# Last output projection with tokens across partitions: the residual turned by VectorE and 128-byte transfers, the norm per partition, token halves in turn

## The chip, the cores and the metric

The kernel runs on one core of one Trainium2 chip. The metric is the device time of one execution in microseconds (us). Five engines work side by side on that core and wait for one another through semaphores: TensorE (PE, with its weight loads as PEld), VectorE (DVE), ScalarE (ACT), GpSimd (POOL, hardly used here) and SyncE (SP), which issues the DMA transfers. All transfers, from whichever queue, are carried by the core's 16 DMA engines.

## What is computed

The reference is a decoder of two blocks on 256 tokens with width 2048, all in float32. The first block has one layer of chunked attention with a relative bias, one layer of attention with forget gates, and an RMS norm. The second block puts 16 meta tokens in front of the 256, normalises, and runs two hybrid layers. The change is at the end of the second of these. Cut to what matters:

```python
def _layer_norm(x, g, b):
    mu = jnp.mean(xf, axis=-1, keepdims=True)
    var = jnp.mean(jnp.square(xf - mu), axis=-1, keepdims=True)
    return (xf - mu) * lax.rsqrt(var + LN_EPS) * g + b

def _hybrid_layer(h, ...):          # h: tokens x 2048
    proj = h @ w_in                 # 2048 x 5632
    ...                             # y_conv 512, y_attn 1024, y_lru 512, each gated
    mixed = jnp.concatenate([y_conv, y_attn, y_lru], axis=-1) @ w_out   # 2048 x 2048
    return _layer_norm(DEEPNORM_ALPHA * h + mixed, ln_post_g, ln_post_b)

for l in range(DEPTH):              # 2 layers
    h = _hybrid_layer(h, ...)
return h[:, N_META:]                # the 16 meta tokens are dropped
```

## The kernel before

**Layout.** The residual stream lies in `X`, two tiles of 128 partitions with eight feature tiles each: features across partitions, tokens along the free axis (`tk(X, m, c0, c1)`, L393, is feature tile m). Every product is made in a split form, for more than the precision of one pass: a float32 operand is cut into a high part (rounded to the fp32r format by ScalarE) and a low part (the rest, by VectorE), and the products high x high, high x low and low x high are added in PSUM. `mm2` (L432) does that with two matmuls when there are 256 tokens: the high weight against high and low tokens side by side (512 columns), and the low weight against the high tokens (256 columns). The two column halves of the 512 wide accumulator are added when it is read.

**The weight stream.** All weights come from one tensor, cut into chunks of 2048 columns, two halves of 1024 each (512 KB). `Prog.run` (L322) writes the order of the work out by hand. For half i it emits, in this order: ScalarE's high part of half i+4 (`high`), VectorE's low part of half i+3 (`low`) and, right after it, the load on SP of half i+7 (`load`, into the buffer which that low part has set free); then the matmuls of half i; then what the chunk that ended before it left to do (`flush`, its evacuation); then one step of each task (`step`). A chunk with `need` first drains the named tasks. Five buffers hold prepared weights (`LOOK` + 2) and four hold raw ones (`RAWB`). Instructions of one engine run in the order in which they are emitted, so a wait holds up all that stands behind it on that engine, SP's queue included.

**Tasks.** The attention, the convolution, the recurrence and the gating are generators that are advanced between the halves. A task that yields `"fill"` is run as filler whenever an estimate of VectorE's clock is less than 2.5 us ahead of TensorE's. `get` and `take` hand out five PSUM banks, `put` gives one back, and three further banks are the accumulators `acc`.

**The last projection (L1705 to L1757, layer 1).** 16 output tiles of 128 features. For the first six the product is cut in two: first the half of the inputs that is ready early (`mix_lo`), for all six, with the pointwise convolution (`pw_mm`) between them, and then the other half (`mix_hi`). The other ten tiles are whole chunks. `ev_o` (L1709) adds the accumulator to the scaled residual, in two passes, and calls `post` of `boundary` (L1045), which subtracts an estimate of the mean, squares, and adds up the sums of the values and of the squares over the feature tiles (`sumd`, `ssum`).

**The end (L1763 to L1791).** The sums go over the partitions by four matmuls with a tile of ones. ScalarE and VectorE make the mean and the inverse deviation as tiles of 128 x 256, the same in each partition. Then every feature tile has its mean subtracted, is multiplied by the inverse deviation (both on VectorE, with groups of two or four tiles in one instruction), and gets the gain and the offset, which lie per partition there, by ScalarE or VectorE. Six stores carry it out.

## Time and profile before

| | us |
|---|---|
| median of 3 runs (2672.63 to 2674.19) | 2673.63 |
| the profiled execution, its own time | 2672.44 |
| span of the profiled execution, first to last instruction | 2670.7 |
| busy in it: PE / DVE / ACT | 2643.2 / 2004.7 / 1501.7 |

The mean granted clock of TensorE is 0.997 of full speed. "Busy" counts the time in which an engine had at least one instruction under way. Matmuls are pipelined, so their times overlap, and the pace is read from start to start. In a row of the timeline the first number is the start in us from the beginning of the span, the second how long the row lasts; `x8` counts merged instructions; a bracket at the end tells how long the engine had stood idle before, and what ended the wait. SPq is SP's queue: the row of a transfer there is its issue and not its flight.

### The profile page before, as it was taken

What the parts mean: (1) busy time and instruction counts of PE and PEld (TensorE: products, weight loads), DVE (VectorE), ACT (ScalarE), POOL (GpSimd) and SP (SyncE); (2) the same over time, 40 slices, a digit from 0 to 9 for tenths busy, and PEclk for the clock granted to TensorE, in tenths of its full rate; (3) what the DMA queues carried; (4) which work ended last, traced back from release to release, by engine and by line L of the source; (5) the groups of instructions that cost most, each with busy time, mean ns of one, the idle gap of its engine ahead of it and who ended that gap; (6) DMA issues with size and microseconds to landing.
All of it is one profiled execution on the core that took longest, in us unless ns stands there. A gap on an engine that the chain in (4) does not pass through costs nothing. (4 is left out here: it accounts for less than half of the span.)

```text
span 2670.7 us, 43856 instructions
## 1 busy us (share of the span) xinstructions
PE 2643.2 (99%) x16914; PEld 2385.1 (89%) x16914; DVE 2004.7 (75%) x3716; ACT 1501.7 (56%) x2326; POOL 3.4 (0%) x20
## 2 busy tenths in 40 slices
PE   9999999999999999999999999999999999999997
PEld 7888888888888888888888888888999999999986
DVE  7777677776765587777777777767799877899867
ACT  6555555555554455554555545644566765756853
POOL 0000000000000000000000000000000000000000
PEclk9999999999999999999999999999999999999998
DMA  7656655555555565555565555565554355554453
GB/s 226 194 175 192 191 176 186 173 192 185 178 181 189 190 199 177 189 177 186 173 193 185 181 185 174 178 203 190 165 186 155 118 164 172 171 172 147 147 171 110
DMA packets 137826, 473.84 MB, mean 177 GB/s; under 512 B 14960, under 2 KB 23568, under 8 KB 137616
## 3 DMA queue, kind: packets, MB, share of 16 engines
q1 hardware_dynamic: 137472, 471.02, 55.2%
q8 instruction: 133, 2.18, 0.3%
q14 instruction: 77, 0.63, 0.1%
q10 hardware_dynamic: 144, 0.01, 0.0%
HBM read 468.84 MB, written 2.13 MB: 176 GB/s over the span
## 5 line engine op out<-in xcount | busy, mean ns | idle before, releaser
L178 ACT CAST w<-raw 128x1024 fp32r<-128x1024 f32 (+1 forms) x874 | 910.5, 1044 | 909.5 <-PE acc L178 661.3
L178 DVE TENSOR_TENSOR w<-raw,w 128x1024 fp32r<-128x1024 f32 (+1 forms) x874 | 1057.0, 1217 | 299.3 <-ACT w L178 298.1
L178 PE MATMUL acc<-hAs1a,w 128*128 128x512 f32 (+1 forms) x768 | 151.7, 339 | 1.1 <-DVE w L178 0.5
L178 PE MATMUL acc<-hAs1b,w 128*128 128x256 f32 (+1 forms) x768 | 150.1, 338 | 1.7 <-DVE w L178 1.7
L178 PE MATMUL acc<-hAs2b,w 128*128 128x256 f32 (+1 forms) x768 | 149.0, 336 | 1.5 <-DVE w L178 1.5
L178 PE MATMUL acc<-hAs2a,w 128*128 128x256 f32 (+1 forms) x768 | 149.7, 337 | 0.0
L178 PEld LDWEIGHTS acc<-hAs1a,w 128*128 128x128 f32 x768 | 122.8, 188 | 18.3 <-DVE w L178 1.8
L178 PEld LDWEIGHTS acc<-hAs2b,w 128*128 128x128 f32 x768 | 123.2, 188 | 17.8 <-issue 1.8
L178 PEld LDWEIGHTS acc<-hAs1b,w 128*128 128x128 f32 x768 | 122.5, 188 | 18.0 <-DVE w L178 2.3
L178 PEld LDWEIGHTS acc<-hAs2a,w 128*128 128x128 f32 x768 | 122.6, 188 | 15.7
L178 ACT ACT_TABLE_LOAD x102 | 130.9, 1283 | 4.4 <-DVE evt L178 1.5
L178 DVE COPY evb<-acc 128x256 f32<-128x256 f32 (+1 forms) x193 | 81.3, 421 | 52.2 <-PE acc L178 52.0
L178 DVE SCALAR_TENSOR_TENSOR rpadw<-agt,pv,rpadw 128x272 f32<-128x272 f32 (+1 forms) x240 | 102.3, 487 | 0.0
L178 PE MATMUL acc<-hbs3b,w 128*128 128x256 f32 (+1 forms) x512 | 100.7, 339 | 0.0
L178 PE MATMUL acc<-hbs3a,w 128*128 128x512 f32 (+1 forms) x512 | 99.6, 337 | 0.0
L178 PE MATMUL acc<-hbs4b,w 128*128 128x256 f32 (+1 forms) x512 | 99.2, 335 | 0.0
L178 PE MATMUL acc<-hbs4a,w 128*128 128x256 f32 (+1 forms) x512 | 99.2, 335 | 0.0
L178 PEld LDWEIGHTS acc<-hbs3a,w 128*128 128x128 f32 x512 | 82.7, 188 | 10.7
L178 PEld LDWEIGHTS acc<-hbs4a,w 128*128 128x128 f32 x512 | 82.5, 188 | 10.9
L178 PEld LDWEIGHTS acc<-hbs4b,w 128*128 128x128 f32 x512 | 82.4, 188 | 10.8
L178 ACT ACTIVATE e<-e,m 128x128 f32<-128x128 f32 (+1 forms) x128 | 57.3, 448 | 61.0 <-DVE m L178 60.7
L178 PEld LDWEIGHTS acc<-hbs3b,w 128*128 128x128 f32 x512 | 81.4, 188 | 10.3
(488 smaller groups left out, 5092.8 us busy)
## 6 DMA issues: line engine op xcount, KB each, us to landing
raw<-in_wstream SPq DMA_DIRECT2D x869, 512.0 KB, 4.4
bias<-in_rel SPq DMA_DIRECT2D x16, 256.0 KB, 5.4
cb<-cumd SPq DMA_DIRECT2D x16, 256.0 KB, 5.0
Xb<-in_xT SPq DMA_DIRECT2D x2, 512.0 KB, 8.4
scrB<-in_lruw SPq DMA_DIRECT2D x2, 512.0 KB, 5.8
tabs<-in_tabs SPq DMA_DIRECT2D x1, 552.0 KB, 6.2
raw<-in_wstream SPq DMA_DIRECT2D x2, 256.0 KB, 5.0
Xa<-in_xT SPq DMA_DIRECT2D x1, 512.0 KB, 7.6
```

The lines of the kernel that those rows point to most:

```text
L178: return fn(*a, **k)
```

## The change

The last projection of the second layer is made with tokens across partitions, in two halves of 128 tokens. The gated inputs become the stationary operand and the weights the moving one, in blocks of 256 output features and two accumulators, one for each token half. For that the residual is turned: `turn_task` transposes every feature tile in blocks of 32 x 32 on VectorE, in place, and `move_task` carries the blocks to their places in a new tile `xt` by 64 transfers from SP, each from 32 partitions to 32 partitions in pieces of 128 bytes; two more transfers copy the gain and the offset into all partitions. An evacuation folds the accumulator into `xt`, takes the mean and variance of its 256 columns with one instruction (`bn_stats`), and multiplies by the gain. The last block of 256 features is computed for the first token half while its weights arrive, and the weights are kept for the second half. At the end mean and deviation are one number per partition; a piece of 512 features takes one pass that makes offset minus mean times gain, and one that applies the deviation. For two pieces of the second half TensorE makes the first of these. The output is stored with tokens across partitions.

The diff, without the unchanged way of layer 0 and the clean-up of `boundary`:

```diff
+    def even(t, c, name):
+        a = slot.tile([P, HS], F32R, tag=t + c, name=name + t + c)
+        off = 48 if c == "b" else 16
+        return a[:, off:off + 4 * 2 * S].rearrange("p (k i n) -> p k i n", k=4, i=2)
...
-                T["M", 2 * i + j] = pairs(sd[i], c, f"mix{i}", L)
+                T["M", 2 * i + j] = even(sd[i], c, "mix") if l else pairs(sd[i], c, f"mix{i}", L)
...
-            pchunk(cq, lambda i=i: T["rg"][:, i, cq:], then=silu_rg if i == 3 else None)
+            pchunk(cq, lambda i=i: T["rg"][:, i, cq:], then=silu_rg if i == 3 else None, spawn=[turn_task] if l and i == 0 else [])
...
-            pchunk(cq, lambda t=t: ag_dst(t), AF.Silu, then=mark(("ag", t)), spawn=[mix_lo, mix_hi] if t == 0 else [])
+            pchunk(cq, lambda t=t: ag_dst(t), AF.Silu, then=mark(("ag", t)), spawn=[mix_lo, mix_hi] if t == 0 else [move_task] if l and t == 7 else [])
...
+    def turn_task():
+        for m in range(16):
+            V.transpose(out=tk(X, m, NM, L), in_=tk(X, m, NM, L))
+            yield "fill"
+
+    def move_task():
+        yield
+        yield
+        last["x"] = [slot.tile([P, HS], F32, tag="s6" + c, name="xt" + c)[:, 0:2048].rearrange("p (t f) -> p t f", t=2) for c in "ab"]
+        for c in range(2):
+            for f in range(4):
+                src = X[c][32 * f:32 * f + 32, :, NM:L].rearrange("p m (t q j) -> p m t q j", t=2, q=4)
+                for q in range(4):
+                    for t in range(2):
+                        dst = last["x"][c][32 * q:32 * q + 32, t].rearrange("p (m f j) -> p m f j", m=8, f=4)
+                        SY.dma_start(out=dst[:, :, f], in_=src[:, :, t, q])
+                yield
+        for k, c in enumerate("ab"):
+            last["gb"[k]] = slot.tile([P, HS], F32, tag="s5" + c, name="row" + c)[:, 0:DM]
+            t = A["rows"]
+            SY.dma_start(out=last["gb"[k]], in_=bass.AP(tensor=t.tensor, offset=t.offset + DM * k, ap=[[0, P], [1, DM]]))
+            yield
...
+        def half_mm(i, t, wt, kt):
+            j, k, m = kt % 4, slice(128 * t, 128 * t + 128), T["M", kt // 4][:, kt % 4]
+            f, e, a = kt == 0, kt == 15, acc[i, t]
+            two = [lambda: TE.matmul(a, m[:, 0, k], wt.both(256 * j, 256), start=f, stop=e),
+                   lambda: TE.matmul(a[:, 256:512], m[:, 1, k], wt.h[:, 256 * j:256 * j + 256], start=False, stop=False)]
+            for x in two if f else two[::-1]:
+                x()
+
+        def mm(i, hh):
+            def f(h, wt):
...
+                if i == 7:
+                    kept.append(wt)
+                for j in range(4):
+                    for t in range(1 if i == 7 else 2):
+                        half_mm(i, t, wt, 8 * hh + 4 * h + j)
+            return f
+
+        def ev(i):
+            def f():
+                for t in range(2):
+                    fold(i, t)
+                    if t:
+                        put(acc[i, t])
+                for t in range(2):
+                    stat(i, t)
+                    gain(i, t)
+            return f
+
+        def fold(i, t):
+            x, a = xt(t, 256 * i, 256), acc[i, t]
+            V.scalar_tensor_tensor(out=x, in0=x, scalar=ALPHA, in1=a[:, :S], op0=ALU.mult, op1=ALU.add)
+            V.tensor_tensor(out=x, in0=x, in1=a[:, S:], op=ALU.add)
+
+        def stat(i, t):
+            V.bn_stats(out=last["bs"][:, t, i], in_=xt(t, 256 * i, 256))
+
+        def gain(i, t):
+            x = xt(t, 256 * i, 256)
+            V.tensor_tensor(out=x, in0=x, in1=last["g"][:, 256 * i:256 * i + 256], op=ALU.mult)
...
+        for i in range(NI):
+            if i == NI - 1:
+                prog.add(Chunk(T["pw_mm"], need=("conv_task",), evac=mark("pw")))
+            add(i, 0, need=("mix_lo",) if i == 0 else ())
+        for i in range(NI):
+            add(i, 1, need=("mix_hi", "move_task") if i == 0 else (), evac=ev(i))
+        for i in range(NI, 8):
+            for hh in range(2):
+                add(i, hh, evac=ev(i) if hh and i < 7 else None)
...
-    b1, b2 = bank(), bank()
...
+    def moments(t):
+        fold(7, t)
+        stat(7, t)
+        V.bn_aggr(out=z[:, t, 0:2], in_=last["bs"][:, t].rearrange("p i c -> p (i c)"))
+        SA.activation(out=z[:, t, 1:2], in_=z[:, t, 1:2], func=AF.Sqrt, scale=1.0, bias=eps[:, 1:2])
+
+    def scales(t):
+        gain(7, t)
+        V.reciprocal(out=z[:, t, 1:2], in_=z[:, t, 1:2])
+        V.scalar_tensor_tensor(out=z[:, t, 2:3], in0=z[:, t, 0:1], scalar=-1.0, in1=z[:, t, 1:2], op0=ALU.mult, op1=ALU.mult)
+
+    def piece(t, c, u=None):
+        w, x = slice(512 * c, 512 * c + 512), xt(t, 512 * c, 512)
+        if u is None:
+            u = B2["wk"].tile([P, 512], F32, tag="pts", name="u", bufs=3)
+            V.scalar_tensor_tensor(out=u, in0=last["g"][:, w], scalar=z[:, t, 2:3], in1=last["b"][:, w], op0=ALU.mult, op1=ALU.add)
+        V.scalar_tensor_tensor(out=x, in0=x, scalar=z[:, t, 1:2], in1=u, op0=ALU.mult, op1=ALU.add)
+        SY.dma_start(out=A["out"][:, t, w], in_=x)
+
+    for kt in range(16):
+        half_mm(7, 1, last["kept"][kt // 4], kt)
+    us = {c: bank() for c in (2, 3)}
+    for c, u in us.items():
+        TE.matmul(u, ident, last["b"][:, 512 * c:512 * c + 512], start=True, stop=False)
+    moments(0)
+    scales(0)
+    for c in range(3):
+        piece(0, c)
+    moments(1)
+    piece(0, 3)
+    scales(1)
+    V.tensor_scalar(out=dg, in0=ident, scalar1=z[:, 1, 2:3], scalar2=None, op0=ALU.mult)
+    for c, u in us.items():
+        TE.matmul(u, dg, last["g"][:, 512 * c:512 * c + 512], start=False, stop=True)
+    for c in range(4):
+        piece(1, c, us.get(c))
```

## Rows read from the trace of the kernel before

**Rows 1.** The page, part 1: busy us (share of span) xinstructions.
```profile
PE 2643.2 (99%) x16914; PEld 2385.1 (89%) x16914; DVE 2004.7 (75%) x3716; ACT 1501.7 (56%) x2326; POOL 3.4 (0%) x20
```

**Rows 2.** Chain that ended last, in order of time: start us, us, what.
```profile
2594.54 55.86 PE acc L178 x320
...
2650.42 0.43 DVE Xb L178
...
2650.88 0.43 DVE Xb L178
...
2665.76 0.32 DVEq L1936
```

**Rows 3.** Timeline, VectorE passes of 256 and 512 columns: start us, us, instruction.
```profile
2614.25 0.42 DVE L178 TENSOR_TENSOR sumd<-sumd,Xa 128x256 f32<-128x256 f32 x1
2614.58 0.42 DVE L178 TENSOR_TENSOR ssum<-ssum,sq 128x256 f32<-128x256 f32 x1
...
2657.15 0.69 DVE L178 TENSOR_TENSOR Xa<-Xa,comb 128x512 f32<-128x512 f32 x1
2657.76 0.69 DVE L178 TENSOR_TENSOR Xa<-Xa,nb 128x512 f32<-128x512 f32 x1
```

**Rows 4.** Groups of VectorE instructions, whole span: xcount | busy us, mean ns.
```profile
L178 DVE TENSOR_TENSOR w<-raw,w 128x1024 fp32r<-128x1024 f32 x866 | 1051.8, 1222 | 296.4 <-ACT w L178 295.2
...
L178 DVE TENSOR_SCALAR anm<-am 128x2 f32<-128x2 f32 x32 | 5.4, 169 | 1.1
...
L178 DVE TENSOR_REDUCE csm<-rpadw 128x256 f32<-128x1024 f32 x1 | 2.0, 1957 | 0.0
...
L178 DVE SCALAR_TENSOR_TENSOR gates<-bank,pv,gates 128x256 f32<-128x256 f32 x4 | 1.9, 484 | 3.3 <-PE bank L178 3.3
```

**Rows 5.** DMA issues by line: xcount, KB each, median us to landing.
```profile
raw<-in_wstream SPq DMA_DIRECT2D x869, 512.0 KB, 4.4
...
out<-Xa SPq DMA_DIRECT2D x2, 256.0 KB, 2.4
```

**Rows 6.** Timeline of SP's queue, two weight loads of the projection's stage.
```profile
2556.51 0.33 SPq L178 DMA_DIRECT2D raw<-in_wstream  x1
...
2561.99 0.33 SPq L178 DMA_DIRECT2D raw<-in_wstream  x1
```

**Rows 7.** Timeline of SP's queue, three of the last issues at the start.
```profile
3.59 0.43 SPq L178 DMA_DIRECT2D Xa<-in_xT  x1
...
4.07 0.69 SPq L178 DMA_DIRECT2D raw<-in_wstream  x1
...
5.61 0.70 SPq L178 DMA_DIRECT2D Xb<-in_xT  x1
```

**Rows 8.** DMA queues in 0:4, 2655:2671, 2600:2625: packets, MB, share of 16 engines.
```profile
q10 hardware_dynamic: 144, 0.01, 2.4%
...
q1 hardware_dynamic: 2144, 2.10, 37.9%
...
q1 hardware_dynamic: 1301, 4.72, 59.3%
```

**Rows 9.** Timeline, TensorE in a v product and the last projection, one fold.
```profile
1126.35 2.94 PE L178 MATMUL accv<-w,hkvs1b 128*128 128x256 f32 x16
...
2577.33 0.95 PE L178 MATMUL acct<-mix1a,w 128*128 128x256 f32 x2 [0.44 <-ACT mix1a L178]
...
2582.43 0.41 DVE L178 SCALAR_TENSOR_TENSOR Xa<-Xa,acct 128x256 f32<-128x256 f32 x1
...
2594.38 1.55 PE L178 MATMUL acc<-mix0a,w 128*128 128x512 f32 x8
```

**Rows 10.** TensorE's last sums; a window after them: busy by engine, PEclk, DMA.
```profile
2652.78 0.59 PE L178 MATMUL bank<-sq,ones 128*128 128x256 f32 x2
...
2657.00:2658.00 1.00, 0.00 (x0) 0.00 (x0) 0.97 (x3) 0.12 (x1) 0.00 (x0) 0.62 0.00 0
```

**Rows 11.** The same view, the stretch between the convolution and the projection.
```profile
2520.00:2551.00 31.00, 30.18 (x248) 27.71 (x248) 24.66 (x29) 26.34 (x46) 0.00 (x0) 1.00 0.46 153
```

More of the change, by code (lines that the diff above doesn't have):

```diff
@@ L1042, in open_block2, with boundary @@
         V.memset(B2["ptm"], 0.0)
-    def boundary(gname, bname, c0, first, move, slots=None, last=False):
+    def boundary(gname, bname, c0, first, slots):
         S_ = {"todo": [], "c": False, "late": []}
@@ L1086, in post @@
         def post(m):
-            if not (last and m == 15):
-                run_late()
+            run_late()
             x = tk(X, m, c0, L)
-            if m == 0 and move:
+            if m == 0:
                 B2["d"] = newp(slots, "d", LW)
@@ L1736, in mm @@
                 for j in range(8):
-                    mm_o(two[m], wt, j, 8 * hh + j, hh == 0 and j == 0, hh == 1 and j == 7)
+                    mm3(two[m][:, :L], wt, j, *msrc(8 * hh + j), hh == 0 and j == 0, hh == 1 and j == 7)
             return mm
@@ L1761, in hybrid_kernel @@
     prog.run()
-    b1, b2 = bank(), bank()
-    for b, u, w in ((b2, sumd[:, NM:], tk(X, 15, NM, L)), (b1, ssum[:, NM:], B2["sq15"][:, NM:])):
-        TE.matmul(b[:, :S], ones, u, start=True, stop=False)
-        TE.matmul(b[:, :S], ones, w, start=False, stop=True)
-    mean, c = (com.tile([P, L], F32, tag=t, name=t)[:, NM:] for t in ("nb", "comb"))
-    SA.activation(out=mean, in_=b2[:, :S], func=AF.Copy, scale=1.0 / DM)
-    SA.activation(out=c, in_=b2[:, :S], func=AF.Square, scale=1.0 / DM)
@@ L1770, in hybrid_kernel @@
[L1770 to L1791 removed]
+    half_mm, fold, stat, gain = last["f"]
```

106 lines of the change are left out of this document (46 added, 60 removed).

## Prediction

> **What bounds the kernel now.** I read the page's busy table first: TensorE is busy for 99% of the span, so a change pays only where TensorE stands still or where something after its last product is shortened [rows 1]. Then the chain of work that ended last: ten output tiles of the last projection run back to back, 320 matmuls in 55.86 us, 5.59 us a tile, up to 2650.40; after that the chain is almost all VectorE, and its last piece ends at 2666.08 [rows 2]. The span ends at 2670.7, so the end after the last product costs 20.3 us: two folds, sums over partitions on TensorE, the reciprocal of a full tile, and 12 wide passes that subtract the mean and multiply. That end is what the change can shorten. Third, the timeline before the end: TensorE waits there only where the gated inputs are made, 0.44 us in the row shown [rows 9], and some 1.2 us with the three short ones beside it.
>
> I count the projection in halves of 1024 weight columns, from half 0 to half 33. Half 14, the first of the later column blocks, starts at 2594.38 [rows 9].
>
> **Part 1: the product itself.** 512 matmuls of 512 or 256 columns stay 512, with tokens now held as weights. The kernel has that form already in its v product: 16 matmuls there take 2.94 us, and 8 of the last projection 1.55 us, each with the drain of its last one counted in [rows 9]; so the same pace. No change: 0. The last block streams its weights in 4 x 1.4 us instead of 4 x 2.8 us, but they are prepared three halves ahead, and the second token half then needs no new weights. The first block of each pass reads the gated inputs in the order that they are made, half a pass later, which can save most of the 1.2 us of waits; the small product for the shift goes too.
>
> **Part 2: turning on VectorE.** 16 transposes of 128x256. No row shows one; a pass over that shape takes between 0.33 us back to back [rows 3] and 0.49 us (a quarter of a 1024-column reduce [rows 4]), so 5 to 8 us, by the nearer row 5.5. They are filler, placed after the convolution's steps, in a stretch where VectorE works 24.66 of 31 us [rows 11]. They cost nothing as long as the splits of the weights stay ahead of TensorE; were that cover gone, at most the 1 to 2 us by which 5.5 us plus a late split exceed the idle.
>
> **Part 3: the transfers, the part that decides.** 64 transfers of 32 KB and two of 1 MB (gain and offset rows) go onto SP's queue, which in this stage issues only one weight load per half. `move_task` is spawned by the last projection chunk, passes two empty steps, and then gives 8 transfers per half: the first group stands behind the load that SP issues at 2556.51, the next behind the one of 2561.99 [rows 6]. Six groups come that way; the last two and the rows are drained at once before half 8. Behind them on SP wait the weight loads of halves 10 to 16.
>
> What does one transfer cost SP? Ahead of one back-to-back run of ten at the start, SP goes from issue to issue in 0.48 us (3.59 to 4.07), but the last three stand 0.77 us apart (4.07 to 5.61 in two steps) [rows 7]; a lone weight load takes 0.33 us [rows 6]. Bounds 0.38 (0.33 and a gap of 0.05) and 0.77. I take 0.47, the pace while the engines are not yet full. The engines: a 64-byte packet took 2.4% of 16 x 4 us / 144 = 10.7 ns, a 1 KB packet 37.9% of 16 x 16 us / 2144 = 45 ns [rows 8]. A transfer is 256 packets and 16 for the semaphore, so 0.18 to 0.77 us; 128 bytes lie nearer to 64, and I take 0.25. A weight load takes 59.3% of 25 us / 9 = 1.65 us [rows 8]. A group and a load then need 8 x 0.25 + 1.65 = 3.65 us of the engines and 8 x 0.47 + 0.38 = 4.1 us of SP: SP is the bound, just.
>
> SP's clock: first group 2556.9 to 2560.7; load; then five times a group and a load of 4.1 us from 2562.4 to 2583; 16 more transfers to 2590.6, and then the gain row. A weight load of 512 KB lands 4.4 us after issue [rows 5]; 512 KB more at the full rate of the stores is 1.4 us (37.9% of 16 us for 2.1 MB [rows 8]). The row lands at 2596.4.
>
> Who waits: `gain(0, 0)`, on VectorE. In the kernel before the first fold of this pass stands at 2582.43 [rows 9]; four folds and one statistic later the multiply would start at 2584.6. VectorE is in order, and behind the multiply stands the low split of half 14. After the row lands come two gains and one statistic (1.2 us) and the split (1.22 us [rows 4]): weights 14 are ready at 2598.8, against 2594.38 now. The next two evacuations (eight passes, 3.4 us each by the durations of part 4) with two splits overrun their 5.6 us slightly, 0.4 us in all. TensorE's end moves by 4.4 + 0.4 = **+4.8 us**. The loads of halves 15 and 16, about 10 us late, land just before that delayed need. At 0.38 us a transfer the row lands at 2592.0 and the shift is +0.4; at 0.77 it lands at 2614.3 and the shift is +22.7.
>
> **Part 4: the end.** T1 is the end of the last token half's product, T0 = T1 - 5.59 that of the first [rows 2]. A dependent pass of 256 columns costs 0.46 us, an independent one 0.33, one of 512 columns 0.61 [rows 2, 3]; a pointer scalar adds 0.06 (484 ns against 420), a tiny instruction 0.17 [rows 4]. The statistic of 256 columns has no row: 0.33 to 0.49, I take 0.45. First half: folds 0.92, statistic 0.45, aggregate 0.17, gain 0.33, root 0.1 beyond it, reciprocal and product 0.34, three pieces of two passes at 1.44: 6.6 us, so VectorE is 1.0 us past T1. Second: 1.54 for its moments, 1.44 for the fourth piece, 0.67 and 0.3 for its scales and the diagonal, two pieces 2.88, and two that TensorE prepared at 0.7: 9.3 us. TensorE's four wide sums lie beside the first two pieces. From the last pass to the span's end it is 4.6 us now [rows 2]; a lone 256 KB store lands in 2.4 us [rows 5], so 3.4 to 4.6, I take 4.0. End 13.3 us (12.4 to 14.2) in place of 20.3: **-7.0 us**.
>
> **Sum.** +4.8 - 7.0 = -2.2 us. The profiled execution took 2672.44 for a span of 2670.7, so 1.7 us lie around it, and the median of the runs is 1.2 us above it. Against the median: 2673.6 - 2.2 = **2671.4**.
>
> **Rivals.** *The rows arrive in time.* If SP needs less than 0.415 us a transfer, or the groups start a half earlier, the row lands before the multiply holds up the splits; then only the end counts, and the saved waits: -5.4 to -8.6, about 2666.5. For it: the stores of the end and a lone load have short issues [rows 6]; against it: every back-to-back issue at the start [rows 7].
>
> *The transfers choke.* One mechanism: issue or packets of the 64 transfers pace at 0.6 us or more, and `gain(0, 0)` holds VectorE, and TensorE with it, until the row lands. It decides from 0.61 us a transfer (net +5.4). At 0.77, the last pace of the start [rows 7], the net is +15.7: 2689. For it: that run of ten slowed after seven; against it: the engines were full with long packets then, and here they have about a tenth to spare. The same follows when a 128-byte packet costs what a 1 KB one does: 0.77 us a transfer, plus the loads, near 1 us, +21 us or more, and I give that 0.08 of the chance.
>
> The Trainium skill (DMA: Bandwidth & Descriptors, Specifications) says that line rate wants transfers of 512 bytes or more, and that below this the engine reads, modifies and writes; by that rule the 128-byte pieces would cost like far longer ones and the last case would hold. The 64-byte row speaks against the worst of it, at 10.7 ns, but it is a load and not a copy within the on-chip memory [rows 8].
>
> *The wait costs the clock.* The clock granted to TensorE stayed full until the window from 2657, where it fell towards half; the last sums on TensorE had started at 2652.78 [rows 10]. A wait of 5 us before half 14 could bring that on; one half at 1.2 GHz instead of 2.4 costs 2.8 us more and leaves the total within 0.2%.
>
> **Chances and range.** A measurement of this kernel can tell about 0.2%, 5.3 us. Forecast and clock case, within 0.2%: 0.42 (own range 2668.3 to 2678.9). Rows in time, faster: 0.36. Choked transfers, slower: 0.22. The range reaches from the whole of the first rival, 2664.5, to 2685, which leaves out the worse half of the second.
>
> **What would show it.** SP's timeline: 64 issues from about 2557 to 2590, pitch 0.47. A wait of VectorE for the transfer of the gain row of about 12 us, once, and right after it a wait of TensorE for `w` of 4 to 6 us; none if the first rival holds, 25 us if the second does. From the last `acc` matmul to the span's end 13.3 us. The prediction is wrong if VectorE waits already in the folds (then the groups start later than I think), if the transposes push the splits, or if the loads of halves 10 to 16 make ScalarE wait before the gain row does.

## Result and the profile after

The changed kernel takes 2690.89 us (median of 6 runs, 2690.16 to 2691.13) against 2673.53 for the kernel before: a ratio of 1.0064 (95% interval 1.0054 to 1.0074), 17.4 us slower. The forecast was 2671.4 with a range to 2685; the time lies outside it. The profiled execution took 2690.83 for a span of 2689.0, 18.3 us more than the span before.

Executions of both kernels differ by a microsecond or two long before the change does anything. The first product of the first layer's output projection, up to which the instructions of both kernels are the same, shows it (timeline of TensorE; columns: start, us, engine, line, operation; kernel before, then after):

```profile
2175.98 1.75 PE L178 MATMUL acct<-mix0a,w 128*128 128x272 f32 x12
```
```profile
2177.97 1.75 PE L176 MATMUL acct<-mix0a,w 128*128 128x272 f32 x12
```

So 2.0 of the 18.3 us are scatter, and I count from this landmark. Three stretches hold the rest: from the landmark to half 0, from there to the end of the product, and the end.

First, TensorE's waits of the changed kernel from 2500 on, then the chain that ended last:

```profile
engine line waited for: us in total, times, longest us
PE acct L176 <- DVE w L176: 8.0, 1, 8.0
PE bank L176 <- ACT pts L176: 7.7, 1, 7.7
PE acct L176 <- DVE mixs3a L176: 5.1, 1, 5.1
PE bank L176 <- DVE dg L176: 3.7, 1, 3.7
```
```profile
2546.22 1.57 ACT rpadw L176 x3
...
2548.84 1.88 ACT w L176 x2
...
2552.20 4.15 PE bank L176 x19
...
2581.07 4.11 DMA raw<-in_wstream
...
2586.91 5.33 DMA raw<-in_wstream
...
2595.11 0.61 SPq L176
...
2610.72 0.61 SPq L176
2611.38 4.84 DMA rowa<-in_rows
...
2617.45 1.23 DVE w L176
...
2664.84 5.58 PE acct L176 x32
```

Where the chain before was TensorE alone up to 2650.42 [rows 2], it now runs through ScalarE, two weight loads, SyncE's issues of the last 24 transfers one after the other (2594.48 to 2611.33, two loads between them) and the gain row. The three large waits are its three breaks; the fourth, for `dg`, lies in the end, where VectorE sets the time.

The stop of 5.1 us (timeline of all engines): SyncE issues a weight load between two groups of transfers; ScalarE waits for it, the cast of the gated inputs stands behind that cast on ScalarE, and TensorE waits for their low part.

```profile
2563.31 5.59 SPq L176 DMA_DIRECT2D xta<-Xa  x8
2569.00 0.54 SPq L176 DMA_DIRECT2D raw<-in_wstream  x1
...
2586.91 1.62 SPq L176 DMA_DIRECT2D raw<-in_wstream  x1
2588.63 5.16 SPq L176 DMA_DIRECT2D xtb<-Xb  x8
2592.35 1.04 ACT L176 CAST w<-raw 128x1024 fp32r<-128x1024 f32 x1 [6.04 <-DMA raw<-in_wstream]
2593.30 0.40 ACT L176 CAST mixs3a<-qt 128x256 fp32r<-128x256 f32 x1
2593.73 0.42 DVE L176 TENSOR_TENSOR mixs3a<-qt,mixs3a 128x256 fp32r<-128x256 f32 x1 [5.83 <-ACT mixs3a L176]
2594.21 1.01 PE L176 MATMUL acct<-w,mixs3a 128*128 128x256 f32 x2 [5.06 <-DVE mixs3a L176]
2595.02 0.84 PE L176 MATMUL bank<-w,mixs3a 128*128 128x256 f32 x2
...
2598.46 0.51 PE L176 MATMUL bank<-w,mixs3b 128*128 128x256 f32 x2
```

Eight transfers take SyncE 5.16 us, 0.645 each (5.59 and 5.53 in the first two groups), and with the load and the gaps a round lasts 5.84 us, for the weights of one half, which TensorE uses up in 2.78 us. The last two kinds of row show what a stop costs besides: pairs of matmuls that are 0.35 us apart afterwards start 0.64 us apart for the first 3 to 4 us, and the granted clock of the stretch from 2590 to 2600 is 0.66 of full.

The stop of 8.0 us: the gain row is issued at 2611.38 and VectorE's first multiply waits for it, with the low split behind it.

```profile
2611.38 0.61 SPq L176 DMA_DIRECT2D rowa<-in_rows  x1
...
2616.31 0.42 DVE L176 TENSOR_TENSOR xta<-xta,rowa 128x256 f32<-128x256 f32 x1 [13.57 <-DMA rowa<-in_rows]
...
2618.72 1.01 PE L176 MATMUL acct<-w,mixs2a 128*128 128x512 f32 x2 [7.96 <-DVE w L176]
```

The end: TensorE starts the sums that it prepares for the last pieces at 2675.81, right behind its last product, and the span ends at 2689.0: 13.2 us. The first sum of the kernel before started at 2650.22, 20.5 us before its end.

All runs in one table, in us. "To half 0" is from the landmark, "product" from there to the start of the first sum behind it, "end" from there to the end of the span; "sum" is all three against the kernel before, and the last column is the time against the kernel before in the same call: the median of 5 to 11 executions for after, thin, thin_late, thin_five, shift_five and shift_four, and one execution for each of the others. The stretches are those of one profiled execution, but they leave out the scatter ahead of the landmark, so single executions are better compared by the sum.

| kernel | to half 0 | product | end | sum | time |
|---|---|---|---|---|---|
| before | 375.1 | 99.1 | 20.5 | | |
| after | 384.4 | 113.4 | 13.2 | +16.3 | +17.4 |
| order_kept | 377.7 | 117.2 | 13.0 | +13.1 | +14.6 |
| order_only | 384.1 | 113.4 | 13.2 | +15.9 | +16.3 |
| rows_first | 383.6 | 112.6 | 13.3 | +14.8 | +17.5 |
| moves_pool | 383.4 | 112.6 | 13.2 | +14.5 | +15.6 |
| moves_128 | 383.8 | 155.8 | 12.9 | +57.8 | +57.5 |
| moves_flat2 | 384.7 | 112.8 | 12.9 | +15.6 | +17.2 |
| moves_forms | 383.8 | 108.5 | 13.2 | +10.8 | +9.7 |
| spread | 384.1 | 97.3 | 12.9 | -0.5 | -0.8 |
| spread_kept | 376.4 | 99.1 | 13.3 | -6.0 | -3.3 |
| spread_noturn | 375.1 | 100.9 | 12.9 | -5.8 | -4.8 |
| thin | 377.6 | 101.4 | 12.9 | -2.8 | -2.3 |
| thin_late | 375.1 | 99.9 | 12.9 | -6.8 | -4.3 |
| thin_five | 375.1 | 102.7 | 12.9 | -4.0 | -4.2 |
| shift_five | 375.1 | 97.3 | 14.7 | -7.6 | -8.3 |
| shift_four | 375.1 | 97.0 | 14.0 | -8.6 | -9.7 |

### The profile page after: what moved, and what is told of

It is laid out like the page before. It is cut to its first block, busy times and chain, and to the rows that moved or that the text cites. A ratio compares the mean times of both kernels' runs of the same rounds, so it can differ in the third digit from the quotient of the medians.

```text
span 2689.0 us, 43875 instructions
## 1 busy us (share of the span) xinstructions
PE 2651.5 (99%) x16912; PEld 2390.5 (89%) x16912; DVE 2002.7 (74%) x3720; ACT 1491.7 (55%) x2297; POOL 3.4 (0%) x20
## 5 line engine op out<-in xcount | busy, mean ns | idle before, releaser
L176 PEld LDWEIGHTS acc<-hbs4b,w 128*128 128x128 f32 x512 | 82.4, 188 | 10.8
```

The lines of the kernel that those rows point to most:

```text
L176: return fn(*a, **k)
```

## Experiments

### The late half 0: work or order

> The changed kernel with one edit: the 16 transposes are issued without being entered in the planner's clock of VectorE, one for each round of its tasks. Every other instruction up to the projection then stands in the order that it has in the kernel before; VectorE still does the 16 transposes. Theory (the planner's order costs the time ahead of the projection): the wait of TensorE for the copy of the probabilities (7.7 us in the changed kernel) and the matmuls at the half clock behind it go, half 0 starts near 2551 us instead of 2562.4, and the time is 2690.9 - 11.3 = 2679.6 us, with 2677 to 2683 as the span. Rival (the 16 transposes themselves, some 6 us of VectorE, push the splits of weights and the attention's small steps): half 0 stays near 2562 and the time within 2 us of 2691.

```diff
-            V.transpose(out=tk(X, m, NM, L), in_=tk(X, m, NM, L))
-            yield "fill"
+            nc.vector.transpose(out=tk(X, m, NM, L), in_=tk(X, m, NM, L))
+            yield
```

> The mirror of the run before: the 16 transposes are entered in the planner's clock of VectorE but not issued, so that every other instruction stands in the order of the changed kernel while VectorE does none of them. The residual's blocks are then not turned: this part of the computation is left out. Theory (the order costs the time): half 0 still starts near 2562 us, the wait of 7.7 us is still there, and the time is 2688 to 2692 us. Rival (the transposes' own time on VectorE): half 0 starts near 2551 and the time is near 2680 us.

```diff
-            V.transpose(out=tk(X, m, NM, L), in_=tk(X, m, NM, L))
+            x = tk(X, m, NM, L)
+            est.start("dve", [x], [x], est.cost("dve", "transpose", x, [x], {}))
             yield "fill"
```

Half 0, with the old order and the transposes (order_kept), then with the new order and none of them (order_only):

```profile
2554.67 0.60 PE L176 MATMUL acct<-w,mixs2a 128*128 128x512 f32 x2
```
```profile
2559.79 0.60 PE L176 MATMUL acct<-w,mixs2a 128*128 128x512 f32 x2
```

From their landmarks (2177.02 and 2175.74) that is 377.7 and 384.1, against 375.1 before and 384.4 after. With spread_noturn below (old order, no transposes: 375.1) the square is full: the order alone costs 9.0 us, the transposes' own work 1.3 to 2.6 in the old order, where they stand from 2445 to 2500, and 0.3 in the new, where most stand from 2513 to 2556. The 1.3 and the 2.6 belong to the same edit. In spread_kept and in order_kept alike TensorE stops for 2.1 us, up to 2534.70 and 2532.58, where it stopped for 0.8 in the kernel before. That is 1.3; the granted clock from 2530 to 2545 is 1.00 in the one and 0.89 in the other, which goes with the rest. The theory on half 0 holds for the order; that the transposes cost something too was not in it. What the order changes is seen on ScalarE (before, then after):

```profile
2536.57 1.08 ACT L178 COPY pts<-bank 128x512 f32<-128x512 f32 x2
2538.72 1.08 PE L178 MATMUL bank<-pts,vt 128*64 128x512 f32 x4
2545.73 2.08 ACT L178 ACTIVATE rpadw<-rpadw,pv 128x256 f32<-128x256 f32 x4
```
```profile
2545.72 2.08 ACT L176 ACTIVATE rpadw<-rpadw,pv 128x256 f32<-128x256 f32 x4 [3.74 <-DVE rpadw L176]
2551.57 1.06 ACT L176 COPY pts<-bank 128x512 f32<-128x512 f32 x2
2552.20 2.45 PE L176 MATMUL bank<-pts,vt 128*64 128x512 f32 x4 [7.68 <-ACT pts L176]
```

The planner, given 16 more steps to fill VectorE with, put the convolution's normalisation ahead of the attention's probabilities; ScalarE, in order, waited 3.74 us for the first, and the copies for which TensorE waited stood behind it.

But the time expected of order_kept, 2679.6, was missed: it took 2686.63, only 2.8 us less (against the kernel before of each call; 3.2 by the sums) where half 0 came 6.7 us earlier. The stop before the gated inputs grew instead, from 5.1 to 7.9 us:

```profile
PE acct L176 <- DVE mixs3a L176: 7.9, 1, 7.9
PE acct L176 <- DVE w L176: 7.2, 1, 7.2
```

In all three kernels TensorE goes on from the second stop about 55 us after SyncE's first transfer: 2563.31 to 2618.72 in the changed kernel, 2558.58 to 2613.91 in order_kept, 2560.74 to 2615.54 in order_only. From there to the end it is 70.3 to 70.9 us in each. SyncE's row of transfers sets the end; an earlier half 0 counts only as far as it lets SyncE start.

### Row, queue or transfers

> The changed kernel with the two loads of the gain and shift rows put ahead of the 64 transfers instead of behind them. Theory (two separate prices behind the start of the projection: the pitch of the transfers on SyncE, which makes the weight loads late, and the gain row behind them, for which VectorE waits 13.6 us and TensorE 8.0): the wait of 8.0 us and about 1.2 us of half clock behind it go, the wait of some 5 us at the second half of the first chunk stays, and the time is about 2690.9 - 9 = 2682 us (2680 to 2684). Rival (the loads are late by so much that TensorE would have stopped there anyway): the stop goes only in part, the waits of ScalarE for weight loads stay at 40 us, and the time is 2686 to 2692 us.

```diff
+        for k, c in enumerate("ab"):
+            last["gb"[k]] = slot.tile([P, HS], F32, tag="s5" + c, name="row" + c)[:, 0:DM]
+            t = A["rows"]
+            SY.dma_start(out=last["gb"[k]], in_=bass.AP(tensor=t.tensor, offset=t.offset + DM * k, ap=[[0, P], [1, DM]]))
         last["x"] = [slot.tile([P, HS], F32, tag="s6" + c, name="xt" + c)[:, 0:2048].rearrange("p (t f) -> p t f", t=2) for c in "ab"]
```

The same lines behind the loop go. Little or nothing was gained: +17.5 in time, 1.5 us less by the sum. The stop of 8.0 us is gone, and the one before it is 9.0 (waits of TensorE, then SyncE's first group, 1.17 us a transfer behind the two megabytes):

```profile
PE acct L176 <- DVE mixs3a L176: 9.0, 1, 9.0
```
```profile
2563.79 9.33 SPq L176 DMA_DIRECT2D xta<-Xa  x8
```

The rival holds (ScalarE still waits 39.5 us for loads), and this tells most about my reasoning: the gain row is one thing for which the transfers make TensorE wait; without it the weight loads, one in 5.84 us, are another.

> The changed kernel with the 64 transfers issued from GpSimd's queue instead of SyncE's; the rows and the weight loads stay on SyncE. Theory (it is the issuing on SyncE, 0.65 to 0.70 us for each transfer, that delays loads and rows): ScalarE's waits for weight loads fall from 40.9 us to below 10, the stops of 5.1 and 8.0 us go with some 2 us of half clock, and the time is about 2690.9 - 15 = 2676 us (2674 to 2679). Rival A (the transfers themselves fill the 16 DMA engines or hold the loads' packets): the loads land as late as before and the time is 2688 to 2692 us. Rival B (issuing on GpSimd is slower than on SyncE): the last transfer lands later than 2612, VectorE waits in the first fold, and the time is above 2692 us.

```diff
-                        SY.dma_start(out=dst[:, :, f], in_=src[:, :, t, q])
+                        nc.gpsimd.dma_start(out=dst[:, :, f], in_=src[:, :, t, q])
```

Rival B in its mechanism, not in its size: 2687.63. GpSimd needs 0.58 us for an issue but pauses between them, and the 64 take from 2556.7 to 2643.2. The stop for the gated inputs is gone, but TensorE waits twice for `w`, 11.3 us in all, behind folds in which VectorE waits for transfers. ScalarE still waits 36.0 us for loads, where the theory said below 10:

```profile
2578.22 1.75 POOL L1764 DMA_DIRECT2D xta<-Xa  x3 [0.96 <-issue]
2583.31 1.75 POOL L1764 DMA_DIRECT2D xta<-Xa  x3 [3.34 <-issue]
```
```profile
DVE xta L176 <- DMA xta<-Xa: 12.6, 1, 12.6
DVE xtb L176 <- DMA xtb<-Xb: 12.6, 1, 12.6
```

What makes GpSimd pause stays open.

### What a transfer costs

> The changed kernel with each of the 64 transfers cut into two of 128 packets (16 KB), so 128 transfers with the same number of packets in all. It asks what sets SyncE's pitch of 0.645 us. If it is the instruction (each transfer has a price of its own, whatever its size): the pitch stays 0.6 to 0.65 us, a group takes 10.3 us, SyncE needs 41 us more, and the time is 25 to 45 us above that of the changed kernel (2715 to 2735). If it is the packets (2.5 ns each): the pitch falls to some 0.33 us, a group still takes 5.2 us, and the time is within 3 us of 2690.

```diff
-                        SY.dma_start(out=dst[:, :, f], in_=src[:, :, t, q])
+                        for m in (slice(0, 4), slice(4, 8)):
+                            SY.dma_start(out=dst[:, m, f], in_=src[:, m, t, q])
```

2730.53 us, 40 us more than the changed kernel: the price is the instruction's. Most groups of 16 take 10.24 to 10.52 us, 0.64 to 0.66 each (the first 11.86). 

> The changed kernel with each of the 64 transfers of 32 KB made plain: 32 partitions with one run of 1 KB each (32 packets) in place of 8 runs of 128 bytes on each. The residual lands in the wrong places: its re-tiling is left out. It asks what makes a transfer cost SyncE 0.645 us where a store of the end costs 0.33 us. If it is the pattern with its many short runs: the pitch falls to 0.35 to 0.45 us, a group and a load take 3.5 to 4.3 us instead of 5.84, the stops of 5.1 and 8.0 us shrink or go, and the time is 2672 to 2680 us. If it is something else (32 partitions, or a copy from the on-chip memory to itself): the pitch stays at 0.6 us or more and the time at 2687 to 2692 us.

```diff
-                        SY.dma_start(out=dst[:, :, f], in_=src[:, :, t, q])
+                        SY.dma_start(out=last["x"][c][32 * q:32 * q + 32, t, 256 * f:256 * f + 256], in_=X[c][32 * f:32 * f + 32, 4 * t + q, NM:L])
```

2689.92 us, +17.2: no gain. Most groups of eight take 4.94 us, 0.62 each. The pattern is not the reason.

> The changed kernel with the same 64 transfers of 32 KB at the same places of SyncE's queue, but of two other forms: the first 32 bring 32 partitions x 1 KB from the device memory (weights, as a stand-in), the last 32 copy 128 partitions x 256 bytes within the on-chip memory. The residual's re-tiling is left out. It asks what is behind the price of a transfer that neither fewer packets nor longer runs lowered: (a) that the source lies in the on-chip memory: the first 32 fall to 0.33 to 0.45 us apart, the last 32 stay at 0.6 or more; (b) that only 32 partitions take part: the other way round; (c) that any issue costs this when another stands right ahead of it on the queue, and the 0.33 us of a lone weight load or store is the price after a pause: both stay at 0.5 us or more, and the time at 2684 to 2692 us. With (a) or (b) SyncE gains some 8 us and the time is 2676 to 2686 us. The theory so far has no preference between them; the run ahead of which two issues at the start of the kernel before stood 0.77 us apart speaks for (c).

```diff
-                        SY.dma_start(out=dst[:, :, f], in_=src[:, :, t, q])
+                        if c == 0:
+                            SY.dma_start(out=last["x"][c][32 * q:32 * q + 32, t, 256 * f:256 * f + 256], in_=A["wstream"][0][32 * f:32 * f + 32, 1024 * t + 256 * q:1024 * t + 256 * q + 256])
+                        else:
+                            n = NM + 64 * q
+                            SY.dma_start(out=last["x"][c][:, t, 256 * f + 64 * q:256 * f + 64 * q + 64], in_=X[c][:, 4 * t + f, n:n + 64])
```

The first 32 have the destination form of moves_flat2, so that against it only the source differs. SyncE's timeline:

```profile
2559.14 3.86 SPq L176 DMA_DIRECT2D xta<-in_wstream  x8
2563.59 0.35 SPq L176 DMA_DIRECT2D raw<-in_wstream  x1
...
2584.62 0.53 SPq L176 DMA_DIRECT2D raw<-in_wstream  x1
2585.20 4.97 SPq L176 DMA_DIRECT2D xtb<-Xb  x8
```

(a) holds, if less sharply than expected: from the device memory 0.48 us apart (3.86 / 8; the other groups 0.49 to 0.53), within the on-chip memory 0.62 (4.97 / 8; the first group, 6.33, was slower). A weight load takes 0.35 us of SyncE behind the first kind and 0.53 behind the second. The stop for the gated inputs is gone and that for `w` is 9.1 us. The sum fits: it is 5.5 us less than in the changed kernel, and SyncE is done with the 64 some 6 us sooner. The time fell by 7.7, of which 2.2 lie outside the three stretches.

### Room on SyncE

> The changed kernel with the 64 transfers thinned out: the 32 that bring the first eight feature blocks go out 5 to a half with the gain row behind the fifteenth, the other 32 and the offset row go out 4 to a half behind half 8 and are needed only before half 20. The order of all compute instructions is that of the changed kernel. Theory (SyncE is full: 8 transfers and a weight load take it 5.84 us where a half lasts 5.56 us; with 5 transfers they take 3.9 us): ScalarE's waits for weight loads fall from 40.9 us to below 12, the stops of TensorE of 5.1 and 8.0 us go, the late start of half 0 stays, and the time is that of the kernel before in the same call + 11.3 - 7.3 = +4 us (+2.5 to +6). Rival (the DMA engines, not the issuing, delay the loads): ScalarE still waits over 20 us for loads and the time is more than 9 us above the kernel before.

```diff
+        yield from move_c(0, 5, 15)
+
+    def rest_task():
+
+        yield from move_c(1, 4, 32)
...
-            add(i, 0, need=("mix_lo",) if i == 0 else ())
+            add(i, 0, need=("mix_lo",) if i == 0 else (), spawn=[rest_task] if i == NI - 1 else [])
...
-                add(i, hh, evac=ev(i) if hh and i < 7 else None)
+                add(i, hh, need=("rest_task",) if (i, hh) == (4, 1) else (), evac=ev(i) if hh and i < 7 else None)
```

`move_c(c, each, row_at)` issues the 32 transfers of one half of the features, `each` per step, and its row behind number `row_at`. 2672.20 us, 17 to 18 us less than the changed kernel (16.8 by the sums, 18.2 by the times) by this one edit, and better than expected (-0.8, not +4). Between half 0 and its last product's end TensorE no longer stops; the one wait left lies in the end (waits from 2555 on):

```profile
PE bank L176 <- DVE dg L176: 3.7, 1, 3.7
```

The product took 97.3 us, 1.8 less than before: the waits for the gated inputs and the product for the shift, which I had put at zero. ScalarE still waited 35 us for loads, against my "below 12", and it cost nothing. By that sign alone the rival would have held; its time, more than 9 us above the kernel before, did not come. This expectation also calls 5.56 us a half; it is a block of two halves, so 3.9 us for a group and a load still fall behind 2.78. The loads lived on the four that are ahead.

> The run before (thinned transfers) and besides the transposes left out of the planner's clock, so that everything up to the projection stands in the order of the kernel before. Theory (two losses that hid each other: with the transfers choking SyncE, an earlier start of the projection only made TensorE wait longer for the loads; freed of that, the earlier start counts in full): half 0 starts 5.1 us later than in the kernel before, the end is 7.3 us shorter, and the time is 2.2 us below the kernel before (0 to 4 below). Rival (the order is worth only the 2.8 us that it gave beside the choke): the time is 1 to 3 us above the kernel before.

> The run before with the 16 transposes not issued at all (neither planned nor done): the residual's 32-column blocks are not turned, so this part of the computation is left out. It prices the transposes' own work on VectorE, by comparison with the run before. Theory (they delay the probabilities' last normalising step by some 2 us, for which TensorE waited 2.1 us, and the split behind it): half 0 starts where it does in the kernel before and the time is 7.3 us below the kernel before (5.5 to 8.5 below), so that the transposes cost 5 us. Rival (they are hidden in VectorE's idle time, as the prediction said): within 1 us of the run before.

```diff
-            V.transpose(out=tk(X, m, NM, L), in_=tk(X, m, NM, L))
-            yield "fill"
+            yield
```

That is the edit of spread_noturn; spread_kept has that of order_kept. Times: -3.3 and -4.8; sums: -6.0 and -5.8. With room on SyncE the old order brings half 0 forward by 7.7 us, but 1.8 go in the product to a new stop of 2.0 us, and the profiled execution was 3.0 us later at the landmark than that of spread, which hides most of the rest in the time. Half 0 is 1.3 us later than in the kernel before, not 5.1. Without the transposes half 0 stands where it did before; the attention's last small step, for which TensorE waits, tells the difference (spread_kept, then spread_noturn):

```profile
2534.70 0.33 PE L176 MATMUL bank<-ident,sc 128*128 128x128 f32 x1 [2.08 <-DVE sc L176]
```
```profile
2531.60 0.33 PE L176 MATMUL bank<-ident,sc 128*128 128x128 f32 x1 [0.84 <-DVE sc L176]
```

The transposes cost 1.3 us to half 0 here, not the 5 expected and not nothing. The 1.5 us between the two times do not show their price: 1.7 us lie ahead of the landmark (2179.14 and 2177.46), and in the product spread_noturn loses 1.8 us more, with a stop of 2.3 us and a granted clock of 0.83 behind it (2580 to 2590).

### Closing the account

> The changed kernel with three edits: transposes outside the planner's clock (order as in the kernel before), transfers 4 to a half (the first 32 ahead of the first evacuation, the other 32 and the offset row behind half 9), gain row behind transfer 28, past the half in which the gated inputs are made. Theory (what is left of the loss once SyncE has room and the order is the old one is the 2 us that the transposes' own work delays half 0): the stop of 2.0 us that stood before the second half of the first chunk, when the gain row's megabyte and 5 transfers a half made one load late, goes; the time is 1.9 - 2.1 (shorter product) - 7.3 (shorter end) = 7.5 us below the kernel before (4.5 to 8 below; the executions scatter by 1 to 2 us ahead of the stage). Rival (loads still late at 4 a half): TensorE stops again for 2 us or more and the time is less than 4 us below.

> The run before with the last 8 of the 16 transposes moved out of the crowded stretch ahead of the projection: each is issued beside a group of transfers, while VectorE is busy for less than half the time. Theory: the probabilities' last normalising step is delayed by 8 transposes less, half 0 starts about 1 us earlier, and the time is 0.5 to 1.5 us below the run before. Rival (a transpose there holds up a split or the gated inputs): a stop of TensorE of 1 us or more appears between halves 1 and 8 and the time is not below the run before.

> The version with 8 early and 8 late transposes, but with the first 32 transfers 5 to a half and the gain row behind transfer 30. With 4 to a half the last transfer of the first 32 was issued late enough for VectorE to wait 6.1 us for it in the first fold, and TensorE stopped for 2.6 us. Theory (with the order, the transposes and SyncE's queue put right nothing else of the change costs TensorE time): no stop of TensorE above 0.5 us from half 0 to the end of the product except none at the fold, half 0 at the same distance from the first layer's projection as in the kernel before, the product 2.1 us shorter and the end 7.3 us shorter: 9.4 us below the kernel before, less the 1 to 2 us by which executions scatter ahead of the stage: 7 to 9.5 us below, a ratio of 0.9964 to 0.9974. Rival (five transfers a half make a weight load late, as in the run where the gain row went out early): a stop of about 2 us moves to the half of the gated inputs and the time is 3 to 6 us below.

```diff
-        yield from move_c(0, 5, 15)
+        yield from move_c(0, 4, 28)
...
                     if k % each == 0:
+                        if c == 0:
+                            m = 7 + k // each
+                            nc.vector.transpose(out=tk(X, m, NM, L), in_=tk(X, m, NM, L))
                         yield
```

The first is an edit of thin against spread, which also has the edit of order_kept, starts `rest_task` one chunk later and drains `move_task` only ahead of the first evacuation (`after=` in place of `need=`). The second is that of thin_late, whose `turn_task` keeps m = 0 to 7; thin_five has `move_c(0, 5, 30)` and two transposes beside each of its first two groups. Ratios: 0.9990 (0.9981 to 0.9999), 0.9986 (0.9976 to 0.9995), 0.9983 (0.9974 to 0.9992). thin and thin_five miss what was expected of them, and their times are in the ranges of the rivals; the stop is not where the rival of thin_five had it. thin_late is 1.9 us below thin, 0.5 to 1.5 expected, and the intervals overlap. The late transposes bring half 0 back to 375.1 us, but a stop remains in each, 2.6 us in thin and thin_late and 3.8 in thin_five, behind VectorE's first fold, which waits for the last of the first 32 transfers (waits of TensorE and VectorE in thin_five):

```profile
PE acct L176 <- DVE w L176: 3.8, 1, 3.8
```
```profile
DVE xta L176 <- DMA xta<-Xa: 5.5, 1, 5.5
```

Not only the issuing makes that transfer late. In all three the last two to four transfers stand right behind the gain row on SyncE, and its megabyte keeps the DMA engines 95 to 98% busy in that moment. The transfers land 4.9 to 6.1 us after their issue, against 2.8 for the first 32 of the changed kernel (medians). A row right behind the 32 was not tried.

> The run before (first 32 transfers 5 to a half, gain row behind transfer 30) with every fold and its statistic issued one block later: the sums of block i are taken out behind block i + 1, and block 6 behind the first token half of block 7; the last 32 transfers go out 3 to a half. A correction to what was expected of the thinned run: a half of 1024 weight columns lasts TensorE 2.78 us, and 5.56 us is a block of two, so 5 transfers and a load (3.9 us of SyncE) still let SyncE fall behind; the loads live on the four that are ahead. Theory (VectorE's wait of 5.5 us for the last of the first 32 transfers, in its first fold, is all that stopped TensorE for 3.8 us): the wait is below 1 us, TensorE has no stop above 1 us before its last product, that product ends 97 to 98.5 us after half 0, the end is 13 to 15 us (one evacuation more lies near it), and the time is 7 to 9 us below the kernel before. Rival (two evacuations close together, or the loads, stop TensorE instead): a stop of 2 us or more and the time no better than 4.5 us below.

> The run before with the first 32 transfers 4 to a half and the gain row behind transfer 28, so that SyncE falls behind by 0.45 us a half instead of 1.1. Theory: the last of the 32 is issued about 3 us later, which the shifted fold still hides; loads are less late; the time is within 1 us of the run before. Rival: with 4 to a half VectorE waits again in the first fold, over 1 us, and the time is 1 to 3 us above the run before.

```diff
-            add(i, 1, need=("mix_hi",) if i == 0 else (), after=("move_task",) if i == 0 else (), spawn=[rest_task] if i == 0 else [], evac=ev(i))
+            add(i, 1, need=("mix_hi",) if i == 0 else (), after=("move_task",) if i == 1 else (), spawn=[rest_task] if i == 0 else [], evac=ev(i - 1) if i else None)
...
-                add(i, hh, need=("rest_task",) if (i, hh) == (4, 1) else (), evac=ev(i) if hh and i < 7 else None)
+                add(i, hh, need=("rest_task",) if (i, hh) == (5, 1) else (), evac=ev(i - 1) if hh and i < 7 else None)
...
+    last["ev"](6)()
     for kt in range(16):
         half_mm(7, 1, last["kept"][kt // 4], kt)
```

`rest_task` now gives 3 transfers to a step; shift_four has `move_c(0, 4, 28)` and one transpose to a group again. 2664.73 us, ratio 0.9972 (0.9963 to 0.9982), and 2663.25 us, ratio 0.9965 (0.9952 to 0.9978): both runs are faster than the kernels before and after, by 0.3% against the one before. In shift_four TensorE does not stop between half 0 and the end of the product, which takes 97.0 us (waits from 2550 on):

```profile
PE bank L176 <- DVE dg L176: 4.3, 1, 4.3
```

Against before: 0.0 to half 0, 99.1 - 97.0 = 2.1 us less in the product, 20.5 - 14.0 = 6.5 us less in the end, together 8.6; measured 9.7, and the difference is within what executions scatter ahead of the landmark. So to within some 1 us nothing else of the change costs time. Between the two paces lie 1.5 us (1.0 by the sums), in favour of 4 to a half, where 1 us was expected, and the intervals overlap; in shift_five the end is 14.7.

## Why the prediction was wrong

**The step that failed** is the +4.8 us of Part 3. TensorE's product ended 23.6 us later than in the kernel before, counted from the landmark. SyncE needed 0.645 us a transfer and not 0.47, it started 4.4 us later, and the weight loads in the same queue stopped TensorE before the gain row did. Part 2, the transposes at nothing, failed with it. The other side of the sum, -7.0, held: -7.3.

**What bounds, and the stop to look for: right.** The end was the place to gain and SyncE the place to lose. VectorE's wait for the gain row (13.6 us, forecast 12) and TensorE's wait for `w` behind it (8.0, forecast 4 to 6) stand where the prediction put them.

**Part 3, the pitch: the term that was mis-sized.** I took 0.47 us a transfer from the issues at the start of the kernel [rows 7]. Those are loads from the device memory (of 128 to 512 KB), and for such transfers, of 32 KB, moves_forms measured 0.48 to 0.53. The 64 are copies within the on-chip memory, at 0.645. The bounds, 0.38 to 0.77, held; the choice fell on the wrong kind of row. From first transfer to gain row SyncE took 48.1 us instead of 33.7: 64 x 0.175 = 11.2; the rest is the first two groups, 0.69 to 0.70 a transfer, and the loads between the groups, 0.54 and once 1.62 us instead of 0.33 [rows 6]. There are seven of these loads, not six: I let the last two groups follow without one. The lower bound has a slip: at 0.38 us the steps as written give a row at 2591.4, not 2592.0.

**Part 3, the start: failed.** The first transfer was issued at 2563.3, not 2556.9; 2.0 us of that is scatter, 4.4 the later start, with half 0 late by the new order. The row landed at 2616.2 instead of 2596.4: 6.4 + 14.4, less 1.0 because it landed in 4.8 us, not 5.8. My own formula (4.8 us of shift for a row at 2596.4) then gives 4.8 + 17.8 = 22.6 us without the scatter; the product's end moved by 25.6 - 2.0 = 23.6.

**Part 3, who waits: half right.** The prediction let only `gain(0, 0)` hold TensorE, and said that the late loads land just in time. At the measured pitch they don't: one load stopped TensorE some 22 us before the row did, through the cast of the gated inputs on ScalarE. The warning in its last lines, that ScalarE might wait for loads first, came true.

**Part 2: failed.** The size was right (0.36 us back to back, 0.39 to 0.45 alone, against 0.33 to 0.49). "They cost nothing" was wrong twice: their own work cost 1.3 to 2.6 us in the old order, a little over the "1 to 2" for the lost cover, and entering them in the planner's clock changed the order of the steps around them, 9.0 us up to half 0. I read how they would be placed and not whom they would displace.

**Part 1: the mis-sized gain.** Taken as 0; the product is 1.8 to 2.1 us shorter where nothing stops it. Rows of the kernel before split it: the 16 matmuls in which it waits for the gated inputs take from 2575.68 to 2579.97, 4.29 us, and the next 16 take 2.78, so the waits are 1.5 us. The shift's product lengthens 2591.14 to 2592.98 to 1.84 us where eight matmuls take 1.39, so it is 0.45.

**Part 4: right, in part by luck.** An end of 13.2 us was measured, 13.3 forecast (12.4 to 14.2). But VectorE's last pass ended 10.2 us behind the product, not 9.3, and from there to the span's end it took 3.0 us, not 4.0 (3.4 to 4.6): two errors of some 1 us that cancel.

**The rivals.** The second, choked transfers, is what happened: it was to decide from 0.61 us, and the pitch was 0.645. Read off its two ends its price there was some 8 us net; the later start (4.4) and the slower loads and groups (some 3) go most of the way from there to the 16.3 by the sums, 17.4 in time. A chance of 0.22 and a range that left out its worse half were too little, since the row behind the forecast was of another kind of transfer. Its other case, that a 128-byte packet costs what one of 1 KB does, did not happen. Where only such copies were under way (2604.5 to 2606.5), 829 packets took the DMA engines 31.8% of 16 x 2 us, 12.3 ns each and 0.21 us a transfer, near the 0.25 forecast and far from 0.77. In moves_flat2 (2603 to 2605) 144 packets, 96 of them of 1 KB, took 18.9%, 0.13 us a transfer. So short pieces cost the engines about 1.7 times as much for the same bytes, and here it is hidden behind SyncE: +17.4 us with them, +17.2 with runs of 1 KB. The Trainium skill (DMA: Bandwidth & Descriptors, Specifications) has transfers under 512 bytes read, modified and written; whether that is behind the 1.7 no run here shows. The same page, in Why small descriptors are slow (HBM only), says that copies from on-chip memory to on-chip memory don't suffer the penalty of short descriptors; the time agrees, the engines' 1.7 does not. The third rival, the clock, came on top: behind both stops TensorE ran 3 to 4 us at about half pace, 3.4 us together (113.4 - 97.0 - 13.0; by the rows 1.8 and 1.5).

## What to carry to other kernels

Price a transfer by a row of the same kind, the same source and the same neighbours on the queue, and compare a group and the load behind it with what the consumer uses up in that time: a queue of loads that falls from one load per 2.78 us to one per 5.84 stops the product whatever else waits. Where an order is planned from costs, an added step that is hidden still moves others; compare the order of the steps, not only the busy time. And while one queue sets the end, removing another loss seems to bring almost nothing (2.8 us of time here, where half 0 came 6.7 us earlier): put the queue right first, then measure the rest.

## What the runs showed of the hardware

- Issuing a 32 KB copy within the on-chip memory from SyncE, back to back, took 0.62 to 0.645 us in most groups whether it had 32, 128 or 256 packets, and on 32 or 128 partitions, and one of 16 KB 0.64 (moves_128); slower groups had 0.66 to 0.93, and the one behind two megabytes 1.17. A transfer of 32 KB from the device memory took 0.48 to 0.53 us. A weight load behind copies on the chip took 0.53 us, behind transfers from the device memory 0.35, alone 0.33.
- On the DMA engines a 128-byte packet of such a copy took 12.3 ns (changed kernel, 2604.5 to 2606.5), and 32 KB in these pieces 0.21 us of the 16 engines, against 0.13 in pieces of 1 KB (moves_flat2, 2603 to 2605).
- Right behind a load of 1 MB the last transfers of thin, thin_late and thin_five landed 4.9 to 6.1 us after their issue, with the engines 95 to 98% busy; the first 32 of the changed kernel took 2.8 (medians).
- From GpSimd each issue took 0.58 us, but 64 of them were spread over 86.5 us.
- After stops of 5.1 and 8.0 us pairs of TensorE's matmuls started 0.64 us apart instead of 0.35 for 3 to 4 us; after the stop of 2.0 us in spread_kept the granted clock from 2580 to 2590 was 1.00, after that of 2.3 us in spread_noturn 0.83. Around the same stop of 2.1 us ahead of the projection it was 0.89 from 2530 to 2545 in order_kept and thin and 1.00 in spread_kept.
- Executions whose instructions are the same up to the landmark reached it at 2174.4 to 2179.1 us in the profiles here, up to 5 us apart.
